# Two runs of fp32 work per retention head, placed in the set order of the main products

## The chip, the cores and the metric

The kernel runs on one core of one Trainium2 chip. The metric is the device time of one execution in microseconds (us); a run's time is compared with others by the median. TensorE is called PE here and in the profile, VectorE DVE, ScalarE ACT, GpSimd POOL, and SP is the queue that issues most transfers.

## The reference, cut to what matters

One layer of a hybrid decoder is computed for a prompt of 256 tokens and for 8 samples of one token each. All 264 columns share the weights. Of its parts the change touches only retention, which has eight heads with 256 q and k features and 512 v features each:

```python
scores = jnp.einsum('bhld,bhmd->bhlm', q, k) * decay[None]
o = jnp.einsum('bhlm,bhmv->bhlv', scores, v) + jnp.einsum('bhld,bhdv->bhlv', q_dec, S)
S_new = jnp.exp(L * log_g)[None, :, None, None] * S + jnp.einsum('bhmd,bhmv->bhdv', k_dec, v)
...
y = (o - mu) * lax.rsqrt(var + GN_EPS)
```

The prompt needs the scores of q and k, their product with v, and a new state from k and v. Each sample needs its old state scaled and updated with its own k and v, and that state's product with its q.

## The kernel before

**The products.** All weights and activations are fp32. Each is split into a high part, rounded to the fast format fp32r, and a low part, the rest; three fp32r matmuls (high by high, high by low, low by high) replace one fp32 product. A chunk is 512 input rows by 256 output columns of weights: a DMA on SP's queue (L204), a cast on ACT (L214), a subtraction on DVE (L215), and 24 matmuls of 264 columns (`gemm_part`, L229). The raw weights have six buffers, the split ones three.

**The order.** The kernel is written with a framework that gives every instruction its engine's queue, allots buffers, and inserts the semaphores. It orders each engine's instructions ahead of time with a simulated timeline, by when their inputs are ready there, and otherwise in the order of the program. [...] `behind(ins, first)` (L183) adds an edge that says only that `ins` is issued after `first` on its engine. `mm` (L194) chains every matmul that goes through it to the one before once `in_order[0]` is true (L527, before the heads), so these stand on PE exactly in the order of the program. A plain `te.matmul` or `te.transpose` has no such edge, and is placed wherever the timeline has its inputs ready.

**The heads.** While head h's retention is worked out, the main products make q, k, v and the gate of head h + 1 (`head_group`, 24 chunks) and project the output of head h - 1 (`project`, 8 chunks): 32 chunks, 24 in head 0, which has nothing to project. In head 7 the chunks of another gate take the place of the next head's. q and k of head h + 1 come first, are rotated on DVE (L552 to L558), and so are complete long before head h + 1 begins. Only head 0 has its rotation at its own start (L753), after the table `rot` has been loaded on POOL's queue (L545).

`retention` returns 19 steps, and `spread` (L90) puts them between the chunks: the first after two chunks, the second after four, the third after six (in head 0 after two, three and four). The last, `gate`, comes after the last chunk, so that the rest of its work falls into the beginning of the next head. The steps that the change touches:

- `sample_rows` (L581): POOL copies the samples' columns of v, sixteen times each, to `vsc`; PE transposes it four times into `vsp` (L587); ACT copies that to `vsr`. `vsc` has the tag `s2` with one buffer, and `head_sum` (L691) uses the same buffer for its sums `s_mu` and `s_var`, which a matmul with ones then adds up over the partitions (L696, `mean_mu`, `mean_var`).
- `scores` (L591): 8 matmuls in full fp32 of k and q into `scp` (L598), a product with the decay on DVE (L600), and the split for the products with v.
- `values` (L604) and `keys` (L614): 8 transposes of v into two tiles `vtp` (L608), 4 of k into `ktp` (L618), with splits by ACT and DVE behind them. All four transposes of k write one bank, and the third and fourth follow the reading of the first two.

The tiles `vsp`, `scp`, `vtp`, `ktp` and `mean_var` are PSUM banks out of a ring of three (`psx`, L147).

Of the kernel before, what the change touches and what calls it, by code (L numbers as in the profile page):

```python
# [25 lines left out]
P = 128  # L26
# [74 lines left out]
def run(steps):  # L101
    for step in steps:
        step()


def call(f, *args):
    return lambda: f(*args)


def together(*steps):  # L110
    return lambda: run(steps)
# [18 lines left out]
def build(ctx, tc, a):  # L130
    nc = tc.nc
    ve, sc, te, sy, gp = nc.vector, nc.scalar, nc.tensor, nc.sync, nc.gpsimd
# [14 lines left out]
    def psx(name):  # L147
        return ps_x[0].tile([P, 512], F32, tag="psx", name=name)
# [15 lines left out]
    ident = cst[:, C_ID:C_ID + P]  # L164
# [18 lines left out]
    def behind(ins, first):  # L183

        tc.add_manual_dep(ins.ins, first.ins.name, mybir.DependencyInfo(
            mybir.DependencyClass.NoSync, mybir.DependencyReason.DATA), reason="issue order")
# [5 lines left out]
    last_mm, in_order = [], [False]  # L192

    def mm(**kw):  # L194

        ins = te.matmul(**kw)  # L196
        if last_mm and in_order[0]:
            behind(ins, last_mm[0])
        last_mm[:] = [ins]
        return ins  # L200

    def raw_chunk(src, name, nk=4):
        w = wts.tile([P, 4, 256], F32, tag="raw", name=name, bufs=N_RAW)
        sy.dma_start(out=w[:, 0:nk, :], in_=src)  # L204
        return w[:, 0:nk, :]
# [19 lines left out]
    def split_act(src, hi, lo):  # L225
        sc.copy(out=hi, in_=src)
        ve.tensor_tensor(out=lo, in0=src, in1=hi.bitcast(F32), op=ALU.subtract)

    def gemm_part(acc, hi, lo, xh, xl, k0, nk, first, last):  # L229

        for b in range(2):
            for k in range(nk):
                cols = slice(b * P, (b + 1) * P)
                s, e = first and k == 0, last and k == nk - 1
                mm(out=acc[:, b, :T], lhsT=hi[:, k, cols], rhs=xh[:, k0 + k, :], start=s, stop=False)
                mm(out=acc[:, b, :T], lhsT=hi[:, k, cols], rhs=xl[:, k0 + k, :], start=False, stop=False)
                mm(out=acc[:, b, :T], lhsT=lo[:, k, cols], rhs=xh[:, k0 + k, :], start=False, stop=e)
# [69 lines left out]
    def mod2_steps(i):  # L307

        mps = []

        def step(k0, n=2, load=raw_chunk, c_in=csil):
            if k0 == 0:
                mps.append(ps_acc.tile([P, 512], F32, tag="mp", name=f"mp2_{i}", bufs=1))
            ws = {(kt, m): load(a["w_mod2"][2 * (i - 2) + m, kt], f"wm2_{i}_{m}_{kt}")
                  for kt in range(k0, k0 + n) for m in range(2)}
            for kt in range(k0, k0 + n):
                for j in range(4):
                    mm(out=mps[0][32 * j:32 * j + 32, :], lhsT=c_in[:, kt, :],
                              rhs=ws[kt, j // 2][:, 2 * (j % 2):2 * (j % 2) + 2, :], start=kt == 0,
                              stop=kt == KT - 1, tile_position=(0, 32 * j))  # L320
            if k0 + n < KT:
                return
            ms = keep.tile([P, 512], F32, tag="ms", name=f"ms2_{i}")
            sc.copy(out=ms, in_=mps[0])
            mt = psx(f"mt2_{i}")
            for b in range(4):
                te.transpose(mt[:, b * P:(b + 1) * P], ms[:, b * P:(b + 1) * P], ident)
            ve.tensor_tensor(out=mod[i].rearrange("p (j b) c -> p b j c", b=4),
                             in0=mt.rearrange("p (b j c) -> p b j c", b=4, j=4)[:, :, :, 0:9],
                             in1=mod_bias(i, slice(0, KT)).rearrange("p (j b) -> p b j", b=4).unsqueeze(3)  # L330
                             .broadcast_to([P, 4, 4, 9]), op=ALU.add)
            if i == SC2:
                k = slice(0, KT)
                fold(SC2, k, mod[i], mod[i])

        return step, [call(step, kt) for kt in range(0, KT, 2)]
# [60 lines left out]
    with tc.tile_pool(name="pooling", bufs=1) as pl:  # L397
# [9 lines left out]
        for i in range(4):  # L407
            k = slice(4 * i, 4 * i + 4)
# [110 lines left out]
        for i in range(N_WARM):  # L519
            m = te.matmul(out=wm[:, 0, 0:P], lhsT=ones, rhs=first_raw[3][:, 0, 0:P], start=True, stop=True)  # L520
# [55 lines left out]
    def retention(h, mods):  # L576

        q, k, v, gr = raw_q[h], raw_k[h], raw_v[h], raw_gr[h]
        st = {}

        def sample_rows():  # L581

            vsc = hp.tile([P, 4, 16, NS], F32, tag="s2", name=f"vsc{h}")
            gp.tensor_copy(out=vsc, in_=v[:, :, TP:T].unsqueeze(2).broadcast_to([P, 4, 16, NS]))
            vsp = psx(f"vsp{h}")
            for i in range(4):
                te.transpose(vsp[:, i * P:(i + 1) * P], vsc[:, i].rearrange("p r b -> p (r b)"), ident)  # L587
            st["vsr"] = hp.tile([P, DV], F32, tag="vsr", name=f"vsr{h}")
            sc.copy(out=st["vsr"], in_=vsp)

        def scores():  # L591

            dec = hp.tile([P, 384], F32, tag="dec", name=f"dec{h}")
            sy.dma_start(out=dec, in_=a["dec"][h])
            scp = psx(f"scp{h}")
            for m0, l0, c0, n in ((0, 0, 0, 256), (P, P, 256, 128)):
                for d in range(2):
                    te.matmul(out=scp[:, c0:c0 + n], lhsT=k[:, d, m0:m0 + P], rhs=q[:, d, l0:l0 + n],  # L598
                              start=d == 0, stop=d == 1)
            ve.tensor_tensor(out=dec, in0=scp[:, :384], in1=dec, op=ALU.mult)  # L600
            st["scs"] = [hp.tile([P, 384], F32R, tag=f"sc{n}", name=f"sc{n}{h}") for n in ("hi", "lo")]
            split_act(dec, *st["scs"])

        def values(m):  # L604

            vtp = psx(f"vtp{h}_{m}")
            for i in range(4):
                te.transpose(vtp[:, i * P:(i + 1) * P], v[:, i, m * P:(m + 1) * P], ident)  # L608
            vh = hp.tile([P, DV], F32R, tag=f"vh{m}", name=f"vh{h}_{m}")
            vl = hp.tile([P, DV], F32R, tag=f"vl{m}", name=f"vl{h}_{m}")  # L610
            split_act(vtp, vh, vl)
            st["vs", m] = vh, vl

        def keys():  # L614
            ktp = psx(f"ktp{h}")
            for m in range(2):
                for d in range(2):
                    te.transpose(ktp[:, m * 256 + d * P:m * 256 + (d + 1) * P], k[:, d, m * P:(m + 1) * P], ident)  # L618
                src, dec = ktp[:, m * 256:(m + 1) * 256], cst[:, C_KD + 2 * h + m:C_KD + 2 * h + m + 1]
                kh = hp.tile([P, DQK], F32R, tag=f"kh{m}", name=f"kh{h}_{m}")  # L620
                kl = hp.tile([P, DQK], F32R, tag=f"kl{m}", name=f"kl{h}_{m}")
                sc.mul(out=kh, in_=src, mul=dec)
                ve.scalar_tensor_tensor(out=kl, in0=src, scalar=dec, in1=kh.bitcast(F32),
                                        op0=ALU.mult, op1=ALU.subtract)
                st["kd", m] = kh, kl
# [82 lines left out]
        def gate():  # L708
# [13 lines left out]
            y[h] = yh, yl  # L722

        return [
            sample_rows, scores, together(call(values, 0), call(values, 1), keys),
            call(sample, 0), call(sample, 1), together(call(prompt_out, 0), call(prompt_out, 1)),
            call(sample, 2), call(sample, 3), together(call(prompt_state, 0), call(prompt_state, 1)),
            call(sample, 4), together(*mods[0:1], call(sample_q, 0)), call(sample, 5), call(sample, 6),
# [26 lines left out]
    for h in range(H):  # L755
        if h + 1 < H:
            head_tiles(h + 1)
            groups = [head_group(h + 1, n) for n in range(6)]
        else:
            groups = [gate_a(g) for g in range(8)]  # L760
        proj = [call(project, h - 1, g) for g in range(8)] if h else []
        mods = later[2 * h:2 * h + 2]
        main = groups[0] + groups[1] + proj[0:4] + groups[2] + proj[4:8] + groups[3] + groups[4] + groups[5]
        run(spread(main, retention(h, mods)))
        for g in groups[6:]:
            run(g)
# [4 lines left out]
    for g in range(8):  # L771
        k = slice(2 * g, 2 * g + 2)
# [50 lines left out]
    with tc.tile_pool(name="res", bufs=2) as rp:  # L823
# [15 lines left out]
        gt2, _ = mod2_steps(GT2)  # L839
# [31 lines left out]
    with tc.tile_pool(name="ffn", bufs=1) as fp:  # L871
# [84 lines left out]
        for g in range(8):  # L956
            k = slice(2 * g, 2 * g + 2)
# [94 lines left out]
```

## Time and profile before

| what | value |
|---|---|
| median of 3 runs | 2267.03 us (2264.86 to 2267.45) |
| the profiled execution's own time | 2261.48 us |
| its span | 2259.7 us, so 1.8 us lie around it |
| PE busy | 2234.2 us, 99% of the span |
| DVE busy | 1505.0 us, 67% |
| ACT busy | 1089.6 us, 48% |
| POOL busy | 222.5 us, 10% |

The span is the time from the first to the last instruction in one profiled execution. A profile lists each instruction with its start and its modelled length. PE's matmuls overlap one another, so what a matmul costs is read from the distance between two starts and not from its length.

### The profile page before, as it was taken

How to read it: one execution, taken by the hardware profiler on the slowest of the kernel's cores; microseconds unless marked ns; L12 is line 12 of the kernel's file. 1: busy time of each engine (PE TensorE's matmuls, PEld its weight loads, DVE VectorE, ACT ScalarE, POOL GpSimd, SP SyncE). 2: the span in 40 equal slices, each digit the busy share in tenths (PEclk: the TensorE clock that was granted, in tenths of full speed). 3: DMA queues.
4: the chain of work that ended last, by engine and by line, in shares of the span. 5: the costliest groups of instructions: out<-in, count | busy, mean ns of one | idle time of the engine just before them, and what ended most of it. 6: DMA issues, size and time to landing. Idle time of an engine off the chain costs nothing.

```text
span 2259.7 us, 44874 instructions
## 1 busy us (share of the span) xinstructions
PE 2234.2 (99%) x18432; PEld 2140.0 (95%) x18432; DVE 1505.0 (67%) x2153; ACT 1089.6 (48%) x1364; POOL 222.5 (10%) x386
## 2 busy tenths in 40 slices
PE   8999999999999999999999999999999999999998
PEld 6899999899999999999999999899999999999998
DVE  6666776686768686877777667676666666654444
ACT  4333454355655555555556554454444444444343
POOL 0000122011101010101010101120000100000000
PEclk9999999999999999999999999999999999999999
DMA  9777867798878787879777879756656666566662
GB/s 337 246 270 261 282 194 274 281 362 315 272 272 287 269 291 253 303 253 321 240 281 264 305 261 349 264 186 187 199 181 216 212 187 215 179 194 190 185 193 100
DMA packets 168254, 561.14 MB, mean 248 GB/s; under 512 B 18448, under 2 KB 28752, under 8 KB 168048
## 3 DMA queue, kind: packets, MB, share of 16 engines
q1 hardware_dynamic: 144048, 474.08, 62.7%
q0 software_dynamic: 23568, 83.73, 10.5%
q8 instruction: 144, 2.36, 0.4%
q14 instruction: 62, 0.51, 0.1%
q10 hardware_dynamic: 432, 0.46, 0.1%
HBM read 509.82 MB, written 48.38 MB: 247 GB/s over the span
## 4 chain that ended last, share of the span: by engine, by line
PE 60%; DVE 1%; DMA 1%; issue 0%; ACT 0%; SPq 0%; DVEq 0%; ACTq 0%
PE acc_up L196 23%; PE acc_dn L196 11%; PE acc_in L196 10%; PE acc_pa L196 4%; PE acc_wo L196 4%; PE acc_ga L196 4%; PE mp L196 1%; PE acc_dn L948 1%; DMA w_in<-in_w_in 1%; PE qp L196 0%; PE scp L598 0%; DMA sgr<-sga_scratch 0%; DVE wl_in L215 0%; DVE wl_pa L215 0%; PE sp L648 0%
## 5 line engine op out<-in xcount | busy, mean ns | idle before, releaser
L196 PE MATMUL acc_up<-h_hi,wh_up 128*128 128x264 f32 x1408 | 400.3, 284 | 0.0
L196 PE MATMUL acc_up<-h_lo,wh_up 128*128 128x264 f32 x1408 | 399.3, 284 | 0.0
L196 PE MATMUL acc_up<-h_hi,wl_up 128*128 128x264 f32 x1408 | 399.0, 283 | 0.0
L196 PE MATMUL acc_in<-h_hi,wh_in 128*128 128x264 f32 x1344 | 386.7, 288 | 0.9 <-ACT wh_in L214 0.8
L196 PE MATMUL acc_in<-h_hi,wl_in 128*128 128x264 f32 x1344 | 381.2, 284 | 1.8 <-DVE wl_in L215 1.8
L196 PE MATMUL acc_in<-h_lo,wh_in 128*128 128x264 f32 x1344 | 382.2, 284 | 0.0
L215 DVE TENSOR_TENSOR wl_up<-w_up,wh_up 128x1024 fp32r<-128x1024 f32 x176 | 216.1, 1228 | 181.2 <-ACT wh_up L214 180.9
L214 ACT CAST wh_up<-w_up 128x1024 fp32r<-128x1024 f32 x176 | 184.6, 1049 | 251.6 <-issue 149.7
L215 DVE TENSOR_TENSOR wl_in<-w_in,wh_in 128x1024 fp32r<-128x1024 f32 x168 | 207.0, 1234 | 130.2 <-ACT wh_in L214 129.1
L214 ACT CAST wh_in<-w_in 128x1024 fp32r<-128x1024 f32 x168 | 176.3, 1049 | 196.3 <-DMA w_in<-in_w_in 94.8
L196 PEld LDWEIGHTS acc_up<-h_hi,wh_up 128*128 128x128 f32 x1408 | 264.8, 188 | 4.2 <-issue 2.5
L196 PEld LDWEIGHTS acc_up<-h_lo,wh_up 128*128 128x128 f32 x1408 | 265.1, 188 | 0.0
L196 PEld LDWEIGHTS acc_up<-h_hi,wl_up 128*128 128x128 f32 x1408 | 264.4, 188 | 0.0
L196 PEld LDWEIGHTS acc_in<-h_hi,wh_in 128*128 128x128 f32 x1344 | 252.9, 188 | 9.5 <-issue 4.2
L196 PEld LDWEIGHTS acc_in<-h_hi,wl_in 128*128 128x128 f32 x1344 | 252.4, 188 | 2.5 <-DVE wl_in L215 2.4
L196 PEld LDWEIGHTS acc_in<-h_lo,wh_in 128*128 128x128 f32 x1344 | 253.0, 188 | 0.7
L196 PE MATMUL acc_st<-h_hi,wh_st 128*128 128x264 f32 x704 | 202.0, 288 | 1.0 <-ACT h_hi L361 1.0
L196 PE MATMUL acc_st<-h_hi,wl_st 128*128 128x264 f32 x704 | 200.2, 285 | 1.4 <-DVE wl_st L215 1.4
L196 PE MATMUL acc_st<-h_lo,wh_st 128*128 128x264 f32 x704 | 200.2, 285 | 0.0
L196 PE MATMUL acc_dn<-f_lo,wh_dn 128*128 128x264 f32 x680 | 192.9, 284 | 0.0
L196 PE MATMUL acc_dn<-f_hi,wl_dn 128*128 128x264 f32 x680 | 192.8, 284 | 0.0
L196 PE MATMUL acc_dn<-f_hi,wh_dn 128*128 128x264 f32 x680 | 192.8, 284 | 0.0
(264 smaller groups left out, 5345.5 us busy)
## 6 DMA issues: line engine op xcount, KB each, us to landing
wm<-in_w_mod SPq DMA_DIRECT2D x176, 512.0 KB, 6.3
w_up<-in_w_up SPq DMA_DIRECT2D x176, 512.0 KB, 3.7
w_in<-in_w_in SPq DMA_DIRECT2D x168, 512.0 KB, 6.0
w_dn<-in_w_down SPq DMA_DIRECT2D x88, 512.0 KB, 3.6
S<-in_state_ret POOLq DMA_DIRECT2D x64, 512.0 KB, 6.3
out_rs<-S POOLq DMA_DIRECT2D x64, 512.0 KB, 6.5
w_pa<-in_w_proj_a SPq DMA_DIRECT2D x64, 512.0 KB, 4.4
w_st<-in_w_in SPq DMA_DIRECT2D x66, 384.0 KB, 4.2
```

The source lines that it names most:

```text
L196: ins = te.matmul(**kw)
L214: c = sc.copy(out=hi, in_=w)
L215: t = ve.tensor_tensor(out=lo, in0=w, in1=hi.bitcast(F32), op=ALU.subtract)
L948: te.matmul(out=accs[b][:, 0, t], lhsT=w[:, k, cols], rhs=f[:, kk, t], start=False, stop=e and not n, skip_group_check=n > 0)
```

## The change

`sample_rows` and `scores` become one step, the first of the head. A new function `turned` makes all twelve transposes of v and k, into three banks, and stands at the head of the second step; `values` and `keys` keep their splits. The third step is empty, so all later steps keep their places. The transposes go through a new helper `turn`, and the score matmuls through `mm`, so both are chained in the set order of the main products. No operation is added or left out.

```diff
--- before.py
+++ after.py
@@ -198,6 +198,13 @@
             behind(ins, last_mm[0])
         last_mm[:] = [ins]
         return ins
+
+    def turn(dst, src):
+
+        ins = te.transpose(dst, src, ident)
+        if last_mm and in_order[0]:
+            behind(ins, last_mm[0])
+        last_mm[:] = [ins]
 
     def raw_chunk(src, name, nk=4):
         w = wts.tile([P, 4, 256], F32, tag="raw", name=name, bufs=N_RAW)
@@ -584,7 +591,7 @@
             gp.tensor_copy(out=vsc, in_=v[:, :, TP:T].unsqueeze(2).broadcast_to([P, 4, 16, NS]))
             vsp = psx(f"vsp{h}")
             for i in range(4):
-                te.transpose(vsp[:, i * P:(i + 1) * P], vsc[:, i].rearrange("p r b -> p (r b)"), ident)
+                turn(vsp[:, i * P:(i + 1) * P], vsc[:, i].rearrange("p r b -> p (r b)"))
             st["vsr"] = hp.tile([P, DV], F32, tag="vsr", name=f"vsr{h}")
             sc.copy(out=st["vsr"], in_=vsp)
 
@@ -595,27 +602,33 @@
             scp = psx(f"scp{h}")
             for m0, l0, c0, n in ((0, 0, 0, 256), (P, P, 256, 128)):
                 for d in range(2):
-                    te.matmul(out=scp[:, c0:c0 + n], lhsT=k[:, d, m0:m0 + P], rhs=q[:, d, l0:l0 + n],
-                              start=d == 0, stop=d == 1)
+                    mm(out=scp[:, c0:c0 + n], lhsT=k[:, d, m0:m0 + P], rhs=q[:, d, l0:l0 + n],
+                       start=d == 0, stop=d == 1)
             ve.tensor_tensor(out=dec, in0=scp[:, :384], in1=dec, op=ALU.mult)
             st["scs"] = [hp.tile([P, 384], F32R, tag=f"sc{n}", name=f"sc{n}{h}") for n in ("hi", "lo")]
             split_act(dec, *st["scs"])
 
+        def turned():
+
+            for m in range(2):
+                st["vtp", m] = psx(f"vtp{h}_{m}")
+                for i in range(4):
+                    turn(st["vtp", m][:, i * P:(i + 1) * P], v[:, i, m * P:(m + 1) * P])
+            st["ktp"] = psx(f"ktp{h}")
+            for m in range(2):
+                for d in range(2):
+                    turn(st["ktp"][:, m * 256 + d * P:m * 256 + (d + 1) * P], k[:, d, m * P:(m + 1) * P])
+
         def values(m):
-
-            vtp = psx(f"vtp{h}_{m}")
-            for i in range(4):
-                te.transpose(vtp[:, i * P:(i + 1) * P], v[:, i, m * P:(m + 1) * P], ident)
+            vtp = st["vtp", m]
             vh = hp.tile([P, DV], F32R, tag=f"vh{m}", name=f"vh{h}_{m}")
             vl = hp.tile([P, DV], F32R, tag=f"vl{m}", name=f"vl{h}_{m}")
             split_act(vtp, vh, vl)
             st["vs", m] = vh, vl
 
         def keys():
-            ktp = psx(f"ktp{h}")
+            ktp = st["ktp"]
             for m in range(2):
-                for d in range(2):
-                    te.transpose(ktp[:, m * 256 + d * P:m * 256 + (d + 1) * P], k[:, d, m * P:(m + 1) * P], ident)
                 src, dec = ktp[:, m * 256:(m + 1) * 256], cst[:, C_KD + 2 * h + m:C_KD + 2 * h + m + 1]
                 kh = hp.tile([P, DQK], F32R, tag=f"kh{m}", name=f"kh{h}_{m}")
                 kl = hp.tile([P, DQK], F32R, tag=f"kl{m}", name=f"kl{h}_{m}")
@@ -722,7 +735,7 @@
             y[h] = yh, yl
 
         return [
-            sample_rows, scores, together(call(values, 0), call(values, 1), keys),
+            together(sample_rows, scores), together(turned, call(values, 0), call(values, 1), keys), together(),
             call(sample, 0), call(sample, 1), together(call(prompt_out, 0), call(prompt_out, 1)),
             call(sample, 2), call(sample, 3), together(call(prompt_state, 0), call(prompt_state, 1)),
             call(sample, 4), together(*mods[0:1], call(sample_q, 0)), call(sample, 5), call(sample, 6),
```

## Rows read from the trace of the kernel before

**Rows 1.** The page's first part: busy time of PE and the others.

```profile
PE 2234.2 (99%) x18432; PEld 2140.0 (95%) x18432; DVE 1505.0 (67%) x2153; ACT 1089.6 (48%) x1364; POOL 222.5 (10%) x386
```

**Rows 2.** Waits of PE, 461 to 1320 us: who, for whom; us, times, longest.

```profile
PE acc_in L196 <- DVE wl_in L215: 1.8, 3, 0.8
PE acc_in L196 <- ACT wh_in L214: 0.8, 1, 0.8
```

**Rows 3.** Stretches of heads 2 and 0: busy by engine, PEclk, DMA share, GB/s.

```profile
659.06:767.80 108.74, 108.74 (x886) 103.67 (x885) 80.99 (x113) 58.72 (x68) 13.24 (x19) 1.00 0.81 278
...
461.70:550.30 88.60, 86.74 (x702) 80.69 (x695) 65.77 (x106) 50.18 (x59) 16.59 (x24) 1.00 0.98 357
```

**Rows 4.** PE's timeline in head 0: start, length, line, tiles, shape, count.

```profile
470.39 0.29 PE L196 MATMUL acc_in<-h_hi,wl_in 128*128 128x264 f32 x1
470.51 0.60 PE L587 MATMUL vsp<-cst,vsc 128*128 128x128 f32 x4
470.87 0.37 PE L196 MATMUL acc_in<-h_hi,wh_in 128*128 128x264 f32 x1
471.08 0.28 PE L196 MATMUL acc_in<-h_lo,wh_in 128*128 128x264 f32 x1
```

**Rows 5.** Timelines of DVE and PE around a wait of PE.

```profile
463.09 1.23 DVE L215 TENSOR_TENSOR wl_in<-w_in,wh_in 128x1024 fp32r<-128x1024 f32 x1 [1.91 <-ACT wh_in L214]
...
464.37 0.39 PE L196 MATMUL acc_in<-h_hi,wl_in 128*128 128x264 f32 x1 [0.76 <-DVE wl_in L215]
```

**Rows 6.** PE's timeline at the beginning of head 2.

```profile
665.24 0.61 PE L696 MATMUL mean_var<-s_var,ones 128*128 128x264 f32 x2
...
665.81 0.28 PE L196 MATMUL acc_in<-h_lo,wh_in 128*128 128x264 f32 x1
...
670.17 0.60 PE L587 MATMUL vsp<-cst,vsc 128*128 128x128 f32 x4
...
671.59 1.47 PE L598 MATMUL scp<-q,k 128*128 128x256 f32 x8
...
678.72 1.04 PE L608 MATMUL vtp<-cst,v 128*128 128x128 f32 x8
```

**Rows 7.** Timelines of DVE and POOL in the same stretch.

```profile
662.01 0.43 DVE L694 TENSOR_TENSOR s_var<-s_var 128x264 f32<-128x264 f32 x1
...
674.85 0.55 DVE L600 TENSOR_TENSOR dec<-scp,dec 128x384 f32<-128x384 f32 x1
...
666.01 0.62 POOL L584 COPY vsc<-v 128x512 f32<-128x512 f32 x1 [24.50 <-ACT wh_in L214]
```

**Rows 8.** Instructions on the tile vsc: ns shortest/median/longest, and a wait.

```profile
L584 POOL COPY vsc<-v x8: 617/618/786, 466.3 to 1211.5; 128x512 f32<-128x512 f32 x8
...
  PE mean_var L696: 23.2, 1
```

**Rows 9.** Timelines of POOL, DVE and PE in head 0.

```profile
465.69 0.58 POOL L545 DMA_DIRECT2D rot<-in_rot  x1 [90.92 <-ACT ms L324]
...
472.94 1.47 DVE L556 SCALAR_TENSOR_TENSOR rot<-q,rot 128x264 f32<-128x264 f32 x4
...
477.61 1.47 DVE L556 SCALAR_TENSOR_TENSOR rot<-k,rot 128x264 f32<-128x264 f32 x4
...
481.11 0.43 DVE L558 TENSOR_TENSOR k<-rot 128x264 f32<-128x264 f32 x1
...
484.04 0.59 PE L598 MATMUL scp<-q,k 128*128 128x256 f32 x2
```

**Rows 10.** The tile rot, 455 to 500 us: its DMA, issue to landing.

```profile
DMA to landing us min/median/max: 7.2/7.2/7.2
```

**Rows 11.** PE's first work, its last, and the stretch after (PEclk 0.50).

```profile
5.04 6.51 PE L417 MATMUL warm_pe<-x,ones 128*128 128x128 f32 x32 [5.04 <-DMA x<-in_xT]
...
2251.37 0.49 PE L798 MATMUL pn_n<-rql_n,ones 128*128 128x132 f32 x2 [0.78 <-ACT rql_n L797]
...
2253.00:2259.70 6.70, 0.00 (x0) 0.50 0.42 163
```

## The prediction

> **What bounds the kernel now.** Read the page's busy times first: PE is busy for 99% of the span [rows 1], the others far less, so time is gained or lost where PE does more, or stands still. Next the waits of PE in the stretch of the eight heads: 2.6 us in some 860 [rows 2]. Then the stretches: in head 2 PE is busy for all of 108.74 us, in head 0 for 86.74 of 88.60, at full granted clock, with the DMA engines at 0.81 and 0.98 [rows 3]. So in the heads PE's work sets the end, and there is almost no waiting that a better order could take away. Any new wait of PE is added to the time in full: nothing behind it is idle.
>
> How long a wait of a matmul lasts is read where one stands now: DVE's subtraction ended at 464.32 (463.09 + 1.23), and the matmul that needed it started at 464.37 [rows 5], 0.05 us later. Nothing of PE ran in between, though further main products stood behind. PE does not pass a matmul that waits. [...]
>
> **What is removed.** The number of matmuls stays. What the closer grouping can save is the passage between fp32r and fp32. From a main product's start to the second one's behind `vsp` (470.39 to 471.08) is 0.69 us for two usual distances of 0.12 and four transposes [rows 4], so the four cost 0.45. Eight transposes last 1.04 and four 0.60 [rows 4, 6], so four more cost 0.44. That leaves 0.01 us for going into fp32 and back. Per head the four runs (`vsp`, `scp`, `vtp` with half of `ktp`, the other half) become two: 2 x 0.01 x 8 = 0.2 us. From above: the first main product behind a run lasts 0.37 instead of 0.29, and the next starts 0.21 behind it instead of 0.12 [rows 4]; counting all 0.09, it is 1.4 us. I take 0.2, since the distances over the whole run are what PE pays. Of the 2.6 us of waits some might go with the new order, all at most; the 0.76 of rows 5 stand before the change acts. I take 0.2 for them, a gain of 0.4 us in all.
>
> **Heads 1 to 7: the transposes of the samples' v.** Now they stand after the head's second chunk whatever happens. Their input `vsc` shares its one buffer with `s_var` of the head before, so POOL's copy waits until `mean_var` has been worked out: one row says so by name [rows 8]. In head 2 that matmul starts at 665.24, just behind the second chunk; POOL copies from 666.01 to 666.63 [rows 6, 7]; and `vsp` starts only at 670.17, since the compiler's order put it there, while main products filled the 4.5 us. With the chain they can't: what is queued behind the waiting transposes on PE is the scores and the third chunk. PE would come to `vsp` as soon as `mean_var`'s two matmuls are through. These and one main product reach from 665.24 to 665.81 [rows 6], so they take 0.45, to 665.69. `vsp` can start at 666.63 + 0.05 = 666.68. PE stands for 1.0 us. `s_var` itself is no obstacle: its sum was ready at 662.44 [rows 7], before the chunk's end. In head 1 the copy has the longest time, 0.79 instead of 0.62 [rows 8], so 1.2 there. Sum over seven heads: 6 x 1.0 + 1.2 = 7.2 us. From below, the wait is nothing if the compiler sets `mean_var` a chunk earlier, which 662.44 would allow; from above it is the whole 670.17 - 665.69 = 4.5, if something else than the copy held `vsp` back, 31 us over seven heads. I take 7.2, as the order up to the second chunk isn't touched and the copy's wait is named in the rows.
>
> **Head 0: the scores.** They now stand right behind `vsp`, which would let them start at 470.95 (470.51 + 0.44). Their k and q come from the rotation, which needs the table `rot`: issued at 465.69, landed 7.2 us later, at 472.89 [rows 9, 10], and the rotation of q began at 472.94 [rows 9]. So PE must stand for 2 us for the landing alone. Then follow, in DVE's order, four products (1.47 long, starts 0.35 apart), two sums (0.34 apart), the same for k: the second half is seen with a split and a shuffle in between, 477.61 to 481.54. Packed, it is 2 x (4 x 0.35 + 2 x 0.34) + 0.1, 4.3 us, so k is ready at 477.3 and the scores start at 477.35: PE stands for 6.4 us. DVE has little to put in between, since the split of chunk 5 wants a buffer that the third chunk, held behind the scores, must free first. From above it is 481.54 + 0.05 - 470.95 = 10.6, if DVE keeps the order of now. I take 6.4, with 0.1 for delays: 6.5 us.
>
> **The clock.** [...] The waits of 1 us in the other heads are about as long as PE's present one before 464.37 (0.76 idle), and the stretch around that shows 1.00 [rows 3, 5]. [...]
>
> **The second run.** Twelve transposes after the fourth chunk need all three banks, and one of them is that of `scp`, which DVE must have read (L600). In head 2 DVE did that 3.3 us after the scores had begun (671.59 to 674.85), and was through at 675.40 [rows 6, 7]. After the change PE would come to the transposes of k at about 675.3: `vsp` from 666.68 and 0.44 long, the scores 1.47 [rows 6], two chunks (48 x 0.12 = 5.8), the eight transposes of v 0.88. DVE should read `scp` sooner than now, as the scores end some 4 us sooner, so I take 0; even at its present time, 675.40, PE would wait 0.15 per head, 1 us in all. That cover is thin, which makes the last rival below. The splits behind come some 3 us earlier than now, and free nothing that PE waits for. SP's and POOL's transfers keep their order; later starts only give them time. The weights for later chunks wait in full buffers after each standstill.
>
> **Sum.** 7.2 + 6.5 + 3.0 - 0.4 = 16.3 us. Against the profiled execution's own 2261.48 it gives 2277.8. That execution was 5.5 us under the median of 2267.03; on the median the time is 2283.3. About 0.2% (4.5 us) is what a measurement of this kernel tells from no change.
>
> **Rivals.**
> - *Nothing to see.* The edges hold nothing back: `mean_var` is set so early that `vsc` is ready at the second chunk's end, and DVE has the rotation of head 0 done earlier. For it speaks that in heads 2 to 7 scores and transposes lie in runs close to these already [rows 6]; against it the landing of `rot`, which alone costs 2 us. With 2 to 4 us left: 2267 + 3 = 2270. Chance 0.12.
> - *Faster.* The passages between the formats are dearer than the distances say, and the standstills don't come. The most that the rows allow is the 1.4 us of passages and the 2.6 of waits: 2267 - 4 = 2263, just short of 0.2%; more would have to come from a better order of DVE and ACT. It decides only if `vsp` waits less than 0.1 us per head. Chance 0.04.
> - *The banks too.* DVE reads `scp` behind the split that follows the third chunk, and the transposes of k wait for it. If DVE's reading slips by one chunk (24 x 0.12 = 2.9 us), PE stands for some 1.9 more in each of seven heads: 13 us, 2296. If the order of DVE makes `vsp` wait the full 4.5 instead, 24 more: 2307. Chance 0.19 for the two, most of it for the first.
>
> **The numbers.** The forecast has 0.65; its own range is 2276 to 2291, from the bounds of the clock (-3.0), of head 0 (+4.1) and of the copy (half to one and a half of 7.2). With one rival on each side the range of 8 in 10 is 2269 to 2299. Slower by over 0.2% are the forecast and the banks: 0.84. Within 0.2%: 0.12; faster: 0.04.
>
> **What the profile of the changed kernel would show.** One gap of PE of 6 to 11 us in head 0 before `scp`, ended by DVE's rotation of k; seven gaps of about 1 us before `vsp`, ended by POOL's `vsc`, each behind `mean_var`; PEclk under 1.00 in the first head's stretch; `vtp` and `ktp` in one run with no gap before `ktp`; PE's sum of matmuls unchanged. I am wrong if `vsp` starts without a gap, or if the gap in head 0 is missing, or if PE's gaps are as I say and the time doesn't follow them.

## The result, and the profile after

The changed kernel takes 2284.82 us (median of 4 runs, 2284.24 to 2288.9), the kernel before 2266.27 beside it (4 runs, 2264.86 to 2267.45): a ratio of 1.0083, 95% interval 1.007 to 1.0097. That is 18.6 us slower. The profiled execution took 2284.57 us, its span is 2282.8.

The two spans differ by 23.1 us, more than the medians do. Head 0's first main product starts at 467.67 us after 463.11 before, so 4.6 us of that lie ahead of the heads, where PE, DVE, ACT and POOL have the same instructions in the same order in both traces. From there to the end of head 7 the changed kernel is 19.6 us longer. Measured from first main product to first main product, head 0 takes 98.40 us instead of 87.20 (the 88.60 of [rows 3] begin 1.4 us ahead of that product), head 1 112.32 instead of 108.75, and the six others some 5 us more together.

The waits of PE between 461 and 1340 us, as [rows 2] (who, for whom; us in all, times, longest):

```profile
PE scp L196 <- DVE k L564: 6.0, 1, 6.0
PE vsp L204 <- POOL vsc L591: 5.8, 7, 0.8
PE acc_in L196 <- ACT wh_in L221: 2.7, 2, 1.5
PE acc_in L196 <- DVE wl_in L222: 2.1, 4, 0.8
PE acc_pa L196 <- ACT v L575: 1.5, 1, 1.5
```

18.1 us instead of 2.6. The first row is one long wait, the second seven short ones, and both name the two late inputs. The last three are main products that wait for their weights or for a bank.

PE's timeline in head 0, as [rows 4, 9], and DVE's beside it:

```profile
475.07 0.60 PE L204 MATMUL vsp<-cst,vsc 128*128 128x128 f32 x4
481.65 2.93 PE L196 MATMUL scp<-q,k 128*128 128x256 f32 x8 [5.98 <-DVE k L564]
484.23 0.57 PE L196 MATMUL acc_in<-h_hi,wh_in 128*128 128x264 f32 x1
...
477.37 1.46 DVE L563 SCALAR_TENSOR_TENSOR rot<-q,rot 128x264 f32<-128x264 f32 x4
478.86 0.43 DVE L564 TENSOR_TENSOR q<-rot 128x264 f32<-128x264 f32 x1
...
479.67 1.46 DVE L563 SCALAR_TENSOR_TENSOR rot<-k,rot 128x264 f32<-128x264 f32 x4
481.16 0.43 DVE L564 TENSOR_TENSOR k<-rot 128x264 f32<-128x264 f32 x1
```

Nothing stands on PE between `vsp` and `scp`. DVE now does both rotations without a split in between. The scores begin at the end of the first of k's two sums (481.16 + 0.43 = 481.59), which gives the half of k that the first of them needs. Behind the wait the eight score matmuls need 2.58 us to the next main product (481.65 to 484.23).

PE's timeline at the beginning of head 2, and POOL's, as [rows 6, 7]:

```profile
684.21 0.61 PE L709 MATMUL mean_var<-s_var,ones 128*128 128x264 f32 x2
685.65 0.66 PE L204 MATMUL vsp<-cst,vsc 128*128 128x128 f32 x4 [0.83 <-POOL vsc L591]
686.14 1.47 PE L196 MATMUL scp<-q,k 128*128 128x256 f32 x8
687.37 0.37 PE L196 MATMUL acc_in<-h_hi,wh_in 128*128 128x264 f32 x1
...
684.99 0.61 POOL L591 COPY vsc<-v 128x512 f32<-128x512 f32 x1 [23.37 <-PE mean_var L709]
```

`mean_var`, POOL's copy, `vsp`: each starts within 0.2 us of the end of the one before, and PE has nothing else that it may do. Here the scores take 1.23 us. The second run, further on in the same head:

```profile
693.26 1.04 PE L204 MATMUL vtp<-cst,v 128*128 128x128 f32 x8
694.14 0.60 PE L204 MATMUL ktp<-cst,k 128*128 128x128 f32 x4
```

Twelve transposes without a gap (0.88 us for the first eight): the banks were free. Stretches of heads 2 and 0, as [rows 3], then the time behind the long wait (busy by engine, PEclk, DMA share, GB/s):

```profile
678.39:788.16 109.77, 108.94 (x886) 103.51 (x885) 80.82 (x113) 58.87 (x68) 13.22 (x19) 1.00 0.78 277
467.67:566.07 98.40, 88.86 (x694) 82.29 (x695) 66.72 (x105) 47.19 (x57) 16.50 (x24) 0.97 0.86 315
481.65:484.95 3.30, 3.30 (x11) 2.94 (x12) 0.62 (x2) 0.00 (x0) 0.00 (x0) 0.50 1.03 397
```

Head 2 takes 109.77 us instead of 108.74, 1.03 more. In head 0 PE worked at a granted clock of 0.50 for the first 3.3 us behind the wait.

### The profile page after: what moved, and what is told of

The parts are those of the page before. It is cut to its first block, busy times and chain, and to the rows that moved or that the text cites. A ratio compares the mean times of both kernels' runs of the same rounds, so it can differ in the third digit from the quotient of the medians.

```text
span 2282.8 us, 44865 instructions
## 1 busy us (share of the span) xinstructions
PE 2239.9 (98%) x18432; PEld 2141.1 (94%) x18432; DVE 1504.5 (66%) x2153; ACT 1088.5 (48%) x1364; POOL 220.8 (10%) x386
## 4 chain that ended last, share of the span: by engine, by line
PE 49%; DVE 1%; DMA 0%; issue 0%; ACT 0%; DVEq 0%; POOL 0%; SPq 0%; POOLq 0%
PE acc_up L196 22%; PE acc_dn L196 11%; PE acc_wo L196 4%; PE acc_ga L196 4%; PE acc_in L196 3%; PE acc_pa L196 2%; PE mp L196 1%; PE acc_dn L961 1%; DVE wl_pa L222 0%; DMA sgr<-sga_scratch 0%; PE qp L196 0%; PE scp L196 0%; DVE y_a L792 0%; DVE m_lo L234 0%; PE sp L661 0%
```

## The experiments

Each is compared with the kernel before, in runs beside it on the same chip. The changed kernel has a ratio of 1.0083, and of 1.0082 when it was run again (the last experiment).

**A buffer of its own for `vsc`.**

```diff
-            vsc = hp.tile([P, 4, 16, NS], F32, tag="s2", name=f"vsc{h}")
+            vsc = keep.tile([P, 512], F32, tag="ms", name=f"vsc{h}").rearrange("p (i r b) -> p i r b", i=4, r=16)
```

(`ms` is a buffer of the modulation steps that is free at that time.)

> The changed kernel with the samples' copy vsc in a buffer that s_var doesn't share, so that POOL can copy before mean_var is worked out. Theory (late inputs of the chained matmuls set the loss, and vsc is one of them): the seven waits of PE before vsp, 0.8 us idle and 1.0 us of the order each, go, so 7 us less, about 2278 us; heads 2 to 7 take 108.7 us each again. Rival (the chain or the passages between fp32r and fp32 cost by themselves): no more than 1 us less, about 2284 us. Rival (the wait is for mean_var or the banks, not for the copy): a wait of the same length before vsp or scp with another releaser, 2282 to 2285 us.

Measured: 2280.41 us beside 2268.99 (6 runs, 2275.34 to 2289.87), ratio 1.005 (1.003 to 1.0069), so 0.0033 or 7.5 us less than the changed kernel, give or take some 5 us by the two intervals. Head 2, its stretch and PE's timeline:

```profile
673.71:782.47 108.76, 108.76 (x887) 103.64 (x886) 80.86 (x113) 58.52 (x68) 13.17 (x19) 1.00 0.80 278
...
679.53 0.61 PE L709 MATMUL mean_var<-s_var,ones 128*128 128x264 f32 x2
679.97 0.60 PE L204 MATMUL vsp<-cst,vsc 128*128 128x128 f32 x4
680.41 1.47 PE L196 MATMUL scp<-q,k 128*128 128x256 f32 x8
```

The order on PE is the same, chained and grouped, and the wait is gone: it was for the copy, and the copy waited for the shared buffer. Head 2 has its 1.0 us back, which is what the prediction put on each of the seven waits. The whole time agrees, but does not settle it: the profiled execution is the quickest of the six, and PE has no late wait for ACT in its head 0 either.

The same trace shows something on head 0's wait, which is 6.0 us here too (rows of POOL and DVE; then the landing of `rot`):

```profile
469.30 0.58 POOL L552 DMA_DIRECT2D rot<-in_rot  x1 [91.69 <-ACT ms L331]
...
476.81 1.23 DVE L222 TENSOR_TENSOR wl_in<-w_in,wh_in 128x1024 fp32r<-128x1024 f32 x1 [0.84 <-ACT wh_in L221]
477.95 1.46 DVE L563 SCALAR_TENSOR_TENSOR rot<-q,rot 128x264 f32<-128x264 f32 x4
...
DMA to landing us min/median/max: 6.1/6.1/6.1
```

`rot` landed at 475.4, and the rotation of q began 2.5 us later, when DVE came to the end of the split of weights ahead of it.

**Head 0 out of the set order.**

```diff
         def scores():
+            free[0] = h == 0
...
-                    mm(out=scp[:, c0:c0 + n], lhsT=k[:, d, m0:m0 + P], rhs=q[:, d, l0:l0 + n],
+                    (te.matmul if free[0] else mm)(out=scp[:, c0:c0 + n], lhsT=k[:, d, m0:m0 + P], rhs=q[:, d, l0:l0 + n],
```

(`sample_rows` and `turned` set the same flag, and `turn` leaves out its edge under it.)

> The changed kernel with the two runs of head 0 alone taken out of the set order; the steps stay grouped, heads 1 to 7 stay chained. Theory: the wait of 6 us for the rotation of k and the low clock behind it go, 7.5 to 8 us; if the later waits of head 0 (3.2 us) and head 1 (1.6 us) for ACT come from the shifted order there, some of these too: 2273 to 2277 us, PEclk 1.00 throughout. Rival (the chain costs the same in each head): an eighth of the loss, about 2282.5 us.

Measured: 2276.29 us, ratio 1.0031 (1.002 to 1.0042): 11.8 us less than the changed kernel, nearly two thirds of the loss from one head of eight. PE's waits for ACT and DVE in the rest of head 0 are gone with the long one. The stretches of heads 0 and 2:

```profile
468.59:557.10 88.51, 87.72 (x694) 82.25 (x695) 65.95 (x106) 48.89 (x58) 16.55 (x24) 0.98 0.95 348
670.65:780.43 109.78, 108.95 (x886) 103.52 (x885) 80.78 (x113) 58.75 (x68) 13.20 (x19) 1.00 0.78 276
```

Head 0 is 9.9 us shorter than after the change (98.40), and head 2 keeps its 1.0. PEclk is not 1.00 throughout as I had expected; that is told at the end.

**A second buffer for the prompt's state.**

```diff
-            so = hp.tile([P, DV], F32, tag="ev", name=f"so{h}_{d}")
+            so = (keep if d else hp).tile([P, DV], F32, tag="ms" if d else "ev", name=f"so{h}_{d}")
```

It was made for a wait that the prediction doesn't have. In the changed kernel's head 0 the rows of POOL, ACT and PE read:

```profile
516.73 0.59 ACT L665 COPY so<-sp 128x512 f32<-128x512 f32 x1 [0.70 <-PE sp L663]
...
525.14 0.72 POOL L671 DMA_DIRECT2D S<-in_state_ret  x1 [10.14 <-DVE wl_in L222]
525.86 0.56 POOL L666 DMA_DIRECT2D out_rp<-so  x1
...
533.12 0.59 ACT L665 COPY so<-sp 128x512 f32<-128x512 f32 x1 [6.31 <-DMA out_rp<-so]
533.60 1.05 ACT L221 CAST wh_in<-w_in 128x1024 fp32r<-128x1024 f32 x1
...
540.36 0.39 PE L196 MATMUL acc_in<-h_hi,wh_in 128*128 128x264 f32 x1 [1.46 <-ACT wh_in L221]
```

`so` has one buffer. Its first half is ready at 517.3, but the store stands in POOL's queue behind a load of `S` that is issued only at 525.14. The second copy waits for the store to land, ACT stands for 6.3 us with the casts of weights behind it, and PE runs out of split weights.

> The changed kernel with a buffer of its own for the second half of the prompt's state (so), so that ACT's copy of it doesn't wait for the first half's store to land. Theory (ACT, held by that copy in heads 0 and 1, casts the weights late): the waits of PE for ACT and DVE in heads 0 and 1, 3.2 and 1.6 us, go; 4 to 5 us less, 2280 to 2281 us; ACT's waits of 6.3 and 5.0 us for the store are gone. Rival (these waits come from the weights' transfers, which a standstill bunches together): waits stay, 2284 to 2285 us.

Measured: 2288.04 us, ratio 1.008 (1.0065 to 1.0096): no gain. ACT's wait is gone, and so are PE's in head 0, which takes 95.5 instead of 98.4 us. But head 1 has a new one (PE's timeline):

```profile
573.82 0.68 PE L709 MATMUL mean_var<-s_var,ones 128*128 128x264 f32 x2 [2.75 <-DVE s_var L707]
575.31 1.11 PE L204 MATMUL vsp<-cst,vsc 128*128 128x128 f32 x4 [0.81 <-POOL vsc L591]
```

With head 0 shorter, PE comes through the second chunk of head 1 before DVE has summed head 0's squares, and stands for `mean_var`, which has its fixed place there. The granted clock falls behind that wait (0.50 from 574.7 to 578.0), and head 1 takes 116.1 instead of 112.3 us. The expected 4 to 5 us were missed; the mechanism of the wait in head 0 holds, the gain was taken back one head later.

**Grouped, not chained.** The flag of the second experiment for all heads (`free[0] = True`).

> The changed kernel with no chain for the two runs in any head: the grouping into two steps and the separate transposes stay. Theory (the fixed places in PE's order are the whole loss): no wait before vsp or scp, 2265 to 2269 us, the time of before within 0.2%. Rival (the closer grouping itself costs, through the three banks held at once or the order of DVE and ACT): 2272 us or more. Rival (grouping saves the passages and the chain hides it): 2262 us or less.

Measured: 2270.54 us beside 2268.99, ratio 1.0005 (0.9995 to 1.0016). The steps stay grouped in the program, and the loss is gone; PE has no wait before `vsp` or `scp`. On PE the second run does not stay together without the chain: in head 2 its transposes start in three groups, at 675.42, 677.07 and 678.48. So this run clears the steps, and the next one the closer runs on PE.

**Grouped and chained, all three waits covered.** The edits of the first three experiments together.

> The changed kernel with all three waits covered at once: head 0's runs out of the set order, vsc in a buffer of its own, the second so in a buffer of its own; heads 1 to 7 keep both runs grouped and chained after the second and fourth chunk. Theory (late inputs are the whole loss, the chain costs nothing): no wait of PE before vsp or scp, heads 2 to 7 take 108.7 us, 2265 to 2269 us, the time of before within 0.2%. Rival (chain or grouping costs by itself): 2272 us or more. Rival (the passages saved are worth something): under 2263 us.

Measured: 2269.83 us beside 2266.0, ratio 1.0016 (1.0007 to 1.0025). Head 2's stretch, with the runs in the order of the changed kernel:

```profile
664.87:773.63 108.76, 108.76 (x887) 103.64 (x886) 80.75 (x113) 58.89 (x68) 13.70 (x19) 1.00 0.81 278
```

108.76 us as against 108.74 [rows 3]: chain and grouping cost a head nothing, and save it nothing. 15 of the 18.6 us are back. The interval of the 0.16% that are left doesn't reach 1; their place isn't shown (in the profiled execution, 2.9 us quicker than the median, head 0 takes 89.36 us instead of 87.20).

**One step later.** Head 0 free, and in heads 1 to 7 both runs after the fourth and sixth chunk; no buffer added.

```diff
-            together(sample_rows, scores), together(turned, call(values, 0), call(values, 1), keys), together(),
+            together(), together(sample_rows, scores), together(turned, call(values, 0), call(values, 1), keys),
```

> Both runs grouped and chained in heads 1 to 7, each one step later (after the fourth and the sixth chunk), head 0's runs out of the set order, all buffers as in the changed kernel. Theory (only the place is wrong: two chunks later vsc is 4.5 us old): no wait before vsp, 2265 to 2269 us, the time of before within 0.2%. Rival (the chain costs wherever it stands): 2275 us. Rival (saved passages show): under 2263 us.

Measured: 2269.62 us beside 2266.0, ratio 1.0012 (1.0002 to 1.0023), 0.6 us above what I expected. PE's timeline at the place:

```profile
679.49 0.60 PE L205 MATMUL vsp<-cst,vsc 128*128 128x128 f32 x4
679.93 1.47 PE L197 MATMUL scp<-q,k 128*128 128x256 f32 x8
```

No wait: the same chain, two chunks later, finds `vsc` ready. So the place was wrong, not the chain. Where the remaining 0.12% lie is not shown.

**The second run alone.** `vsp` and `scp` as before the change; only the twelve transposes chained, after the sixth chunk (the fourth in head 0).

```diff
-            together(sample_rows, scores), together(turned, call(values, 0), call(values, 1), keys), together(),
+            sample_rows, scores, together(turned, call(values, 0), call(values, 1), keys),
```

> The second run alone: samples' v and scores unchained and in the two steps of before, the twelve transposes of v and k chained after the sixth chunk (the fourth in head 0). Theory (the second run's banks and inputs are ready, it costs nothing in heads 1 to 7; in head 0 the transposes of k come after four chunks, some 5 us before the rotation of k is done): heads 1 to 7 as before, head 0 with one wait of 3 to 5 us and perhaps a drop of the clock, 2269 to 2274 us. Rival (the banks held at once cost in each head): waits before vtp or ktp in heads 1 to 7, 2275 us or more.

Measured: 2275.31 us beside 2266.0, ratio 1.0044 (1.0032 to 1.0056), 1.3 us beyond the range that I expected and at the time of the rival, but without the rival's waits. PE in head 0:

```profile
485.57 1.22 PE L605 MATMUL scp<-q,k 128*128 128x256 f32 x2 [4.26 <-DVE k L564]
...
491.21 0.66 PE L204 MATMUL ktp<-cst,k 128*128 128x128 f32 x4 [1.72 <-DVE vl L234]
```

The transposes of k want the rotated k as the scores do, and hold the main products behind them for it; here `ktp` waits for its bank as well (1.7 us). In heads 1 to 7 no wait stands before `vtp` or `ktp`. But head 1 shows a wait of 2.0 us for ACT at a projection, which I had not expected, and this execution, the slowest of the five (2280.01), has the granted clock at 0.50 in three stretches of 3.4 us.

**PE kept at work in head 0's wait.** Matmuls without use between `vsp` and the scores:

```diff
+            if h == 0:
+                fill = psx("fill")
+                for _ in range(50):
+                    mm(out=fill[:, 0:P], lhsT=ones, rhs=ident, start=True, stop=True)
```

> The changed kernel with 50 fp32 matmuls of 128 columns without use, on constants, chained between vsp and the scores of head 0, so that PE works (50 x 0.11 = 5.5 us) while it waits for the rotation of k. Theory (PE's standstill brings the clock down, and that costs half of the 3.3 us that PE then works at the lower level): PEclk stays 1.00 behind the wait, the scores and chunk after them are 1.6 us faster, head 0 takes about 96.8 instead of 98.4 us; 1.6 us less in all, 2283 us. Rival (the clock would cost the 3.0 us of the prediction): 2282 us. Rival (it falls whatever PE does, or the matmuls delay the scores): no change or 1 to 5 us more.

Measured: 2288.49 us, ratio 1.0098 (1.0085 to 1.0111). I had sized it wrongly: these became 100 instructions 0.112 us apart, 11.2 us in all, and the scores started at 487.92, 5.1 us after the sum of k that they need was there (482.41 + 0.43). So with 26:

> The run with matmuls without use in head 0's wait once more, with 26 of them: each full fp32 matmul of 128 columns turned out as two instructions 0.112 us apart, so 50 of them took 11.2 us and delayed the scores; 26 take 5.8 us and fit into the wait of 6.2. Theory: scores start when k is rotated, as in the changed kernel, the granted clock stays 1.00 behind the wait, and PE has the 1.6 us back that the eight score matmuls and the first main products lost at 0.5: head 0 takes 1.6 us less than in the changed kernel beside it, about 2283 us. Rival (the clock costs the 3.0 us of the prediction): 3 us less. Rival (the clock falls all the same): no gain.

Measured: 2284.54 us beside 2266.12, ratio 1.008 (1.0067 to 1.0093); in the whole time 0.1 us less than the changed kernel run again beside it (2284.62), so the expected 1.6 us don't show there, and the interval is too wide to rule them out. The place itself speaks (PE's timeline; then the stretch's PE busy, PEclk, DMA share, GB/s):

```profile
478.20 5.97 PE L196 MATMUL fill<-cst,ones 128*128 128x128 f32 x52
484.36 1.57 PE L196 MATMUL scp<-q,k 128*128 128x256 f32 x8 [0.19 <-DVE k L564]
485.69 0.37 PE L196 MATMUL acc_in<-h_hi,wh_in 128*128 128x264 f32 x1
...
478.00:486.00 8.00, 7.81 (x66) 1.00 1.03 399
```

The clock stays at 1.00, and the scores take 1.33 us instead of 2.58. So at this place the low clock went with the standstill: 0.50 behind 5.98 us of it, 1.00 behind 0.19. Head 0 is 94.7 us long, 3.7 less than after the change. That is not the clock's worth alone: PE's waits for ACT and DVE behind the scores are missing too, and against it the clock fell at the head's beginning (0.50 from 470.3 to 473.6), where the changed kernel kept 1.00. Head 1 is 1.3 us longer.

**Two buffers, head 0 chained.** The edits of the first and third experiments.

> The changed kernel, all heads chained, with the buffers of its own for vsc and for the second so together. Theory: what is left is head 0's wait for the rotation of k with the low clock behind it, 6.3 and 1.6 us; heads 1 to 7 as before; since vsp no longer comes behind mean_var, the late s_var of head 1 that stood in the way with the second so alone doesn't hold PE: 2274 to 2276 us. Rival (ACT's and DVE's late splits in heads 0 and 1 come from the standstill in head 0 and not from the store): waits for ACT of 2 us or more remain there, 2277 to 2280 us.

Measured: 2280.97 us beside 2266.12 (6 runs, 2276.19 to 2286.68), ratio 1.0073 (1.0059 to 1.0087). The profiled execution is the quickest of the six, 2276.19, next to the expected 2274 to 2276; the median is not. The wait of PE for `s_var` in head 1 is there again, 2.8 us, ahead of `mean_var`, although `vsp` no longer hangs on it. Nothing shows where the others lose 5 us more. My expectation failed in both.

**The changed kernel again.**

> The changed kernel itself once more. Theory: one wait of 6.2 us before the scores of head 0, seven of 1.2 us from start to start before vsp, and ACT held by the store of so in heads 0 and 1 with 3 to 5 us of waits of PE behind it, since all these are set by the fixed order; 2283 to 2288 us. Rival (the waits behind ACT are of that one execution): they are missing or lie elsewhere.

Measured: 2284.62 us beside 2266.12, ratio 1.0082 (1.0069 to 1.0095). Its waits of PE:

```profile
PE scp L196 <- DVE k L564: 6.1, 1, 6.1
PE vsp L204 <- POOL vsc L591: 5.8, 7, 0.8
PE acc_in L196 <- DVE wl_in L222: 2.6, 4, 0.8
PE acc_in L196 <- ACT wh_in L221: 1.5, 1, 1.5
```

The two late inputs are the same to a tenth, and ACT's wait for the store in head 0 is 6.1 us after 6.3. The wait of 1.5 us in head 1 is missing, so that one is not fixed by the order. The low clock lasts longer into PE's work than the first time (the stretch, as [rows 3]):

```profile
480.90:485.63 4.73, 4.73 (x18) 4.37 (x19) 1.41 (x3) 0.51 (x1) 0.00 (x0) 0.50 1.03 400
```

## Why the prediction was right, and where a size was off

**PE sets the end, and does not pass a waiting matmul.** Held: PE waits 15.5 us more (18.1 after 2.6), and the heads take 19.6 us more. In the 5.98 us before the scores of head 0 no matmul starts on PE, with the next chunk's main products standing behind them.

**The samples' v, 7.2 us.** Right in place, releaser and size: 1.03 in head 2, seven rows of 0.8, and 7.5 in all when the shared buffer is taken away. The idle time in the row is 0.83; most of the other 0.2 is the end of `mean_var`'s modelled length, 0.61, where the next start could come 0.44 behind. The longer copy that was to add 0.2 in head 1 did not come again (0.61 us); the 0.03 more in each head make up for it.

**Head 0, 6.5 us.** Right in size and releaser: the scores start 6.25 us behind the last transpose, which usually takes 0.11, so 6.1. DVE did rotate q and k without a split between them, as the packed sum assumed. The first step of that sum, that the landing of `rot` starts the rotation, is not borne out, and that it gave the right time is luck: in the changed kernel `rot` lands at 477.15 (470.25 + 6.9) and the split of weights ahead of the rotation ends at about the same time (476.22 + 1.23). In the first experiment the landing came 2.5 us ahead of the rotation and the wait was still 6.0. By this, loading `rot` earlier would not by itself have shortened it; no run tried that.

**The clock, 3.0 us.** The drop is shown, 0.50 from 481.65 to 484.95, but the term was too large. The scores lost 1.35 (2.58 less the 1.23 of head 2), the next three main products 0.3 (0.78 from 484.23 to 485.01, usually 0.45): 1.7 us. The price is not fixed: when the changed kernel was run again, PE's work met 4.7 us of the low stretch instead of 3.3, main products started 0.22 us apart instead of 0.12, and some 2.3 us were lost. No run shows the 3.0 us of the sum; the runs show these 1.7 and 2.3 us in its place. The 3.0 were my estimate from the 32 matmuls at the start, 6.51 us [rows 11], and the profile's granted clock reads 1.00 there, whatever made those matmuls slow:

```profile
5.04:11.55 6.51, 6.50 (x36) 1.00 1.03 412
```

With the 26 matmuls without use (52 instructions) PEclk was 1.00 between 478 and 486, instead of 0.57.

**The gain of 0.4 us.** Not there: a head with both runs and no wait takes 108.76 as against 108.74.

**The second run, nothing.** Right in the changed kernel, no gap before `ktp`; the rival of the banks fell. Where the run stands behind late scores, a wait for its bank does come (1.7 us in the seventh experiment told).

**What I left out.** "SP's and POOL's transfers keep their order; later starts only give them time" was wrong for POOL's queue. The order changed: before, two stores of `S` (485.94, 487.26) stood ahead of head 0's fifth load of `S` (491.15), after the change one (493.73 ahead of 497.95). And the store of `so` behind a held load held ACT in head 0, so that main products waited for split weights. From the heads' first main product on, main products wait 5.1 us for ACT and DVE in the profile of after and 4.1 when it was run again, 1.8 before: 2.3 to 3.3 us more.

Sum of what was measured: 7.2 + 6.1 + 1.7 + 3.3 = 18.3 us in the first profile, 7.2 + 6.1 + 2.3 + 2.3 = 17.9 in the second, for 19.6 and 19.7 us in the heads; the other 1.3 to 1.8 us have no place. That the forecast of 16.3 came so near the 18.6 of the medians owes something to two errors of opposite sign, the clock (0.7 to 1.3 too much) and the late main products (2.3 to 3.3 left out).

## What to carry to other kernels

In this kernel an edge that fixes PE's order was free where the inputs were old (108.76 us a head as against 108.74), and cost the time by which they came late where they were not (0.83 us for `vsc` in head 2, 5.98 for k in head 0). Before a step goes into a set order, look up in the trace when its latest input is ready and what shares a buffer with it; moved by two chunks, or with its inputs early, and with head 0 left out, the same chain cost 0.1 to 0.2% instead of 0.8%. And grouping the formats was worth no more than the distance between starts says of the passage, 0.01 us a time.

## What was not expected of the hardware

The granted clock also fell behind shorter waits, in some executions and not in others. With head 0 free, PE waited 1.50 and 0.75 us at the beginning of head 0, and then:

```profile
468.59 0.39 PE L197 MATMUL acc_in<-h_hi,wh_in 128*128 128x264 f32 x1 [1.50 <-ACT wh_in L224]
...
469.85 0.39 PE L197 MATMUL acc_in<-h_hi,wl_in 128*128 128x264 f32 x1 [0.75 <-DVE wl_in L225]
...
470.90:474.30 3.40, 3.40 (x18) 3.40 (x17) 0.79 (x4) 1.30 (x2) 3.13 (x5) 0.50 0.98 383
```

PE was busy for all of these 3.4 us, at 0.50. In the changed kernel 1.2 and 0.8 us of waits at the same place left it at 1.00. The length of these waits doesn't decide it: in the first experiment 1.2 and 0.8 us were followed by 0.50 (468.7 to 472.0), and with the two buffers 1.9 and 0.8 us by 1.00. What does is not shown. At half the clock such a stretch costs some 1.7 us (an estimate, half of the row's 3.40 us); it may be one reason why single executions of one kernel differ, which no run settles.

A full fp32 matmul of 128 columns stands in the trace as two instructions 0.112 us apart (the 50 matmuls without use are 100 from 476.75 to 487.92), while a transpose of the same size is one, 0.11 behind the last (eight in 0.88 us). So the eight score matmuls of a head are four of the program, and the 32 at the start are sixteen; the distances between starts, and the sums made of them, stay the same.
